# Feed-forward activations turned by 32x32 blocks on VectorE and two DMAs through DRAM instead of on TensorE

## The chip, the cores and the metric

The kernel runs on one core of one Trainium2 chip. The metric is the time of one execution on the device in microseconds (us). A core has TensorE (PE, matrix multiplication, with weight loads listed as PEld), VectorE (DVE), ScalarE (ACT), GpSimd (POOL) and SyncE (SP); each runs its instructions in the order in which the program wrote them, and waits on semaphores where it needs what another engine or a transfer (DMA) delivers. The memories on the core are SBUF (128 partitions) and PSUM (eight banks of 128x512 fp32, into which TensorE writes).

## The reference

Two transformer blocks of width 2048 over 256 tokens, fp32 throughout, within tight tolerances. Attention, a recurrence and the rest of the blocks are cut here; the change touches the two feed-forward parts. Both have 5632 inner features:

```python
# first block
gate, up = jnp.split(h @ w_gate_up[layer], 2, axis=-1)
x = x + rms_norm((jax.nn.silu(gate) * up) @ w_down[layer], g_ffn_post[layer])
...
def conv_ffn(h, w_up, conv_w, conv_b, w_down):     # second block, CONV_WIDTH = 3, L = 256 tokens
    ...
    u = h @ w_up
    up = jnp.pad(u, ((0, 0), (CONV_WIDTH - 1, 0), (0, 0)))
    acc = conv_b
    ...
        acc = acc + conv_w[j] * up[:, j:j + L]
    ...
    return (jax.nn.silu(gate) * val) @ w_down
```

## The kernel before

**Matrix products.** The tokens are two tiles of 128 (t = 0, 1). A product of activations with a weight is cut into chunks of 512 output columns. Its weight comes from DRAM in half-pieces of 512 KB (two blocks of 128 rows by 512 columns), which SP's queue loads into a staging tile `stg`. Fp32 accuracy comes from splitting each operand into a high and a low part: ACT casts the high part of the half-piece into a tile of the `ring` (L278), DVE subtracts it from the staged weight and writes the low part (L285), and PE runs 12 matmuls of 128x512 on it (L331): two blocks, three passes (high by high, high by low, low by high), two token tiles. The activations are stored transposed (features on partitions, tokens along the row), since TensorE contracts over the partitions; the result in PSUM has tokens on the partitions. So between the up product and the down product the activation has to be turned.

**Feed-forward part of the first block.** `ffn` runs gate and up chunks in turn, 11 of each, in six groups: the four chunks of acts 0 and 1, those of acts 2 and 3, then the down product of group 0 (four chunks), then the next group, and so on. `ffn_gate` writes silu of the gate to SBUF; `ffn_up` multiplies the up result with it on DVE (L1017), one 128x512 tile per token tile. Four PE transposes of 128x128 (`transposes`, L346) put the turned tile into a PSUM bank of class `sd`; `evac_split` takes it from there as high part (ACT, L352) and low part (DVE, L353).

**Feed-forward part of the second block.** `ffn2` has the same groups with 22 chunks `conv` (gate and value for each of 11 acts). `two` evacuates both token tiles of a chunk to SBUF on ACT (L1214). Then `conv` fills two `sd` banks with four PE transposes each (L1534), and does the convolution along the row of tokens: ACT writes one tap and the bias (L1541), DVE adds the other two taps (L1542, L1543). Gate chunks end with a Silu on ACT (L1546). Value chunks are multiplied with the gate on Pool (L1560), cast on ACT (L1563), and the low part is subtracted on Pool (L1564).

**What sets the order.** One planner writes the program. It lists all matmul steps with planned times, and before each step it issues the casts of the half-pieces that fall due within 12 us (`AHEAD_HI`), the subtractions within 11 us (`AHEAD_LO`), and the loads that have a staging place. The work between products is written as generators that advance by one `yield` per 1.4 us of planned time (`TICK`); `yield 3` waits for three ticks. So the order on each engine is fixed by planned times, and at run time semaphores alone decide. The down chunk's step waits in the plan until its activation is marked ready. Transfers other than weights go out on Pool's queue (`self.mq`). Small tiles of 128x512 (`s2`) are quarters of pages in SBUF. During act 1's gate chunk of the first feed-forward part a generator `prep_t5` loads two small tables (L483, L484), multiplies them on PE (L486) and spreads the result over 2 MB of DRAM (L490).

Of the kernel before, what the change touches and what calls it, by code (L numbers as in the profile page):

```python
# [8 lines left out]
F32 = mybir.dt.float32  # L9
# [9 lines left out]
P = 128  # L19
# [16 lines left out]
B_LEAD = ((1, 2), (4, 3), (3, 3))  # L36
B_STEP = 2
LO_LAG = 2
NEG = -1.0e30
EPS = 1e-6  # L40

# [38 lines left out]
class Core:  # L80
# [267 lines left out]
    def evac_split(self, bank, hi, lo, scale=None):  # L348

        nc = self.nc  # L350
        if scale is None:
            nc.scalar.copy(hi, bank)  # L352
            nc.vector.tensor_tensor(lo, bank, hi.bitcast(F32), op=ALU.subtract)  # L353
        else:
            nc.scalar.activation(hi, bank, AF.Copy, scale=scale)
            nc.vector.scalar_tensor_tensor(lo, bank, scale, hi.bitcast(F32), op0=ALU.mult, op1=ALU.subtract)

    def x_block(self, src, xt, j, t, goff):

# [16 lines left out]
        def low():  # L376
            yield LO_LAG
            for a in range(4):
                nc.vector.scalar_tensor_tensor(lo[:, a], b3[:, a], g[a], hi[:, a].bitcast(F32), op0=ALU.mult, op1=ALU.subtract)  # L379
            self.put("sd")  # L380
            xt.ready.add((j, t))
# [627 lines left out]
    def ffn_up(self, c, i):  # L1009
        ps = c.ps  # L1010
        nc = self.nc

        def done(t):
            while (i, t) not in self.half:
                yield 1
            g = self.half.pop((i, t))
            nc.vector.scalar_tensor_tensor(g, ps[t], self.rs[t], g, op0=ALU.mult, op1=ALU.mult)  # L1017
            self.put("mm")
            a = self.act[i]
            yield 1  # L1020
            if a.blk[0] is None:
                a.blk[0] = True
                a.blk[0] = yield from self.get("s8", dt=F32R)
            while a.blk[0] is True:
                yield 1
            yield 2
            bank = yield from self.get("sd")
            self.transposes(bank, [g[:, b * P : (b + 1) * P] for b in range(4)])
            self.drop(g)
            s = slice(t * P, (t + 1) * P)  # L1030
            self.evac_split(bank.rearrange("p (k n) -> p k n", k=4), a.hi(0)[:, :, s], a.lo(0)[:, :, s])
            self.put("sd")
            a.ready.add((0, t))
        return done

# [238 lines left out]
    def topk(self):  # L1274
# [11 lines left out]
        for t in range(2):  # L1286
# [3 lines left out]
            for it in range(8):  # L1290
# [3 lines left out]
                if it % 2:  # L1294
                    yield 1
            nc.vector.tensor_scalar(wk, wk, -3.0e38, -NEG, op0=ALU.is_equal, op1=ALU.mult)
            nc.vector.tensor_scalar(wk, wk, NEG, None, op0=ALU.add)
            nc.vector.tensor_tensor(wk[:, n - P : n], wk[:, n - P : n], self.cm[:, P:256], op=ALU.add)
# [225 lines left out]
    def conv(self, c, i, gate):  # L1524
        nc = self.nc
        b0 = 4 * i + (0 if gate else 44)

        def then(got):
            outs = []
            for a in range(2):  # L1530
                bank = yield from self.get("sd")
                for b in range(2):
                    for t in range(2):
                        nc.tensor.transpose(bank[:, (2 * b + t) * P : (2 * b + t + 1) * P],  # L1534
                                            got[t][:, (2 * a + b) * P : (2 * a + b + 1) * P], self.ident)
                o = yield from self.get("s2")
                for b in range(2):
                    k = b0 + 2 * a + b
                    w = [self.cols[:, C_CW + 88 * z + k : C_CW + 88 * z + k + 1] for z in range(3)]
                    u, v = bank[:, 256 * b : 256 * b + 256], o[:, 256 * b : 256 * b + 256]  # L1540
                    nc.scalar.activation(v, u, AF.Identity, scale=w[2], bias=self.cols[:, C_CB + k : C_CB + k + 1])  # L1541
                    nc.vector.scalar_tensor_tensor(v[:, 1:], u[:, 0:255], w[1], v[:, 1:], op0=ALU.mult, op1=ALU.add)  # L1542
                    nc.vector.scalar_tensor_tensor(v[:, 2:], u[:, 0:254], w[0], v[:, 2:], op0=ALU.mult, op1=ALU.add)  # L1543
                self.put("sd")
                if gate:
                    nc.scalar.activation(o, o, AF.Silu)  # L1546
                    self.half[i, a] = o
                outs.append(o)
                yield 1
            self.drop(got[0], got[1])  # L1550
            if gate:
                return
            act = self.act[i]
            act.blk[0] = yield from self.get("s8", dt=F32R)
            for a in range(2):
                while (i, a) not in self.half:
                    yield 1
                g = self.half.pop((i, a))
                o = outs[a]
                nc.gpsimd.tensor_tensor(o, o, g, op=ALU.mult)  # L1560
                o3 = o.rearrange("p (k n) -> p k n", k=2)
                hi, lo = act.hi(0)[:, 2 * a : 2 * a + 2, :], act.lo(0)[:, 2 * a : 2 * a + 2, :]
                nc.scalar.copy(hi, o3)  # L1563
                nc.gpsimd.tensor_tensor(lo, o3, hi.bitcast(F32), op=ALU.subtract)  # L1564
                self.drop(o, g)
                yield 1
            act.ready |= {(0, 0), (0, 1)}
        return self.two(c, then)

    def last_out(self, c, j):  # L1570
# [360 lines left out]
def _pieces(np, w, n=512):  # L1931
    k = w.shape[0]
    return np.ascontiguousarray(w.reshape(k // 256, 2, 128, -1, n).transpose(3, 0, 2, 1, 4))


def _shape_constants(np):
# [12 lines left out]
    c_pick = np.concatenate(picks + [u == pos], axis=1).astype(np.float32)  # L1949
    ninf = np.float32(NEG)  # L1950
    prev = np.where(pos > u, np.float32(0), ninf)
# [15 lines left out]
def _layout(np, a):  # L1967
    heads = [0, 4, 1, 5, 2, 6, 3, 7, 8, 12, 9, 13, 10, 14, 11, 15]
    w_in = a["w_in"][0]
    aq = w_in[:, 0:1024].reshape(2048, 16, 64)[:, heads].reshape(2048, 1024)  # L1970
    w2 = a["w_in_2"][0]

    def cols(v):
        return v.reshape(-1, 128).T

    conv_w = a["conv_w_2"][0]
    vectors = [a["g_mix_pre"][0], a["g_ffn_pre"][0], a["g_ple_pre"][0], a["norm1_g_2"][0], a["norm2_g_2"][0],
               a["kv_norm_g_2"][0], a["hgrn_gnorm"][0], a["conv_b_2"][0], conv_w[0], conv_w[1], conv_w[2]]
    r = {
        "x": a["x"][0], "p": a["p"][0, 0], "pos": np.ascontiguousarray(a["positions"][0].reshape(2, 128).T),  # L1980
        "cols": np.concatenate([cols(v) for v in vectors], axis=1),
        "rv": np.concatenate([a["attn_sinks"][0][heads], a["fgate_b_2"][0]]),
        "lbl": np.ascontiguousarray(a["hgrn_lb_logits"].reshape(2, 8, 128).transpose(2, 0, 1).reshape(128, 16)),
        "w_in": _pieces(np, np.concatenate([aq, w_in[:, 1024:]], axis=1)),
        "w_ab": _pieces(np, a["w_attn_branch"][0].reshape(16, 64, 2048)[heads].reshape(1024, 2048)),
        "w_hb": _pieces(np, a["w_hgrn_branch"][0]),
        "w_out": _pieces(np, a["w_out"][0]),
        "w_gu": _pieces(np, a["w_gate_up"][0]),
        "w_dn": _pieces(np, a["w_down"][0]),
        "w_pg": _pieces(np, a["w_ple_gate"][0]),  # L1990
        "w_pp": _pieces(np, a["w_ple_proj"][0]),
        "w_in2": _pieces(np, np.concatenate([w2[:, 0:1024], w2[:, 1280:2304], w2[:, 2384:5456]], axis=1)),
        "w_sm": _pieces(np, np.concatenate([w2[:, 1024:1280], w2[:, 2304:2384], w2[:, 5456:5464]], axis=1), 344)[0],
        "w_uk": _pieces(np, a["w_uk_2"][0].transpose(2, 0, 1).reshape(256, 1024)),
        "w_uv": _pieces(np, a["w_uv_2"][0].transpose(1, 0, 2).reshape(256, 1024)),
        "w_o": _pieces(np, a["w_o_2"][0]),
        "w_up2": _pieces(np, a["w_up_2"][0]),
        "w_dn2": _pieces(np, a["w_down_2"][0]),
        "g_mix_post": a["g_mix_post"][0], "g_ffn_post": a["g_ffn_post"][0], "g_ple_post": a["g_ple_post"][0],
        "g_fin": a["final_g_2"], "t5": a["t5_table_2"],  # L2000
    }
    r.update(_shape_constants(np))
    return {k: np.ascontiguousarray(v) for k, v in r.items()}
# [16 lines left out]
```

## Time and profile before

| | us |
|---|---|
| three runs | 2701.66, 2703.8, 2704.35 |
| median of the runs | 2703.8 |
| profiled execution, its own time | 2698.83 |
| span of the profiled execution | 2696.8 |

The core's mean granted TensorE clock over the span was 0.997 of full speed. The profile lists each engine's busy time; a group of instructions is one line of the program with one form, and `out<-in` are the program's tiles (`mm` and `sd` are PSUM banks, `s` a tile in SBUF, `ring` the split weights, `stg` the staged ones, names that begin with `d_` are DRAM). The first feed-forward part lies at 707 to 1380 us, the second at 1950 to 2640 us.

### The profile page before, as it was taken

To read this page: it belongs to the slowest core of one execution; us is meant where nothing else is said; L and a number is where in the kernel's file an instruction comes from. 1 tells how busy PE (TensorE), PEld (TensorE's weight loads), DVE (VectorE), ACT (ScalarE), POOL (GpSimd) and SP (SyncE) were. 2 spreads that over 40 slices of the span, in tenths; PEclk is the share of its full clock that TensorE was granted. 3 is DMA by queue.
4 is the path that set the end of the run, shared out by engine and by line. 5 is a ranking of instruction groups with operands and counts; after the bars stand their busy time and mean duration, and the time that the engine had idled before them with its cause. 6 is when DMAs were issued, how large, how long until landed. Compare 5 with 4: busy or idle time off the path is not lost. (4 is left out here: it accounts for less than half of the span.)

```text
span 2696.8 us, 32408 instructions
## 1 busy us (share of the span) xinstructions
PE 2656.7 (99%) x12193; PEld 2194.9 (81%) x12193; DVE 1559.6 (58%) x2063; ACT 1310.5 (49%) x1916; POOL 312.5 (12%) x298
## 2 busy tenths in 40 slices
PE   8999999999999999999999999999999999999998
PEld 7887788888778888888887778788888888888887
DVE  6865675465635445454557564855555646464656
ACT  6545644454525443434345564555455535353634
POOL 1341031021200000000002310100001101020101
PEclk9999999999999999999999999999999999999999
DMA  7445446667576555555557555455555555555553
GB/s 252 164 144 165 152 154 200 218 230 262 197 182 227 191 195 193 193 197 193 192 176 241 206 211 179 146 178 198 187 181 189 185 189 185 190 194 181 195 180 132
DMA packets 144539, 513.97 MB, mean 191 GB/s; under 512 B 17688, under 2 KB 20272, under 8 KB 143360
## 3 DMA queue, kind: packets, MB, share of 16 engines
q1 hardware_dynamic: 133504, 476.83, 51.0%
q0 software_dynamic: 9584, 34.50, 4.2%
q8 instruction: 95, 1.56, 0.2%
q10 hardware_dynamic: 1296, 0.59, 0.1%
q14 instruction: 60, 0.49, 0.1%
HBM read 497.16 MB, written 14.70 MB: 190 GB/s over the span
## 5 line engine op out<-in xcount | busy, mean ns | idle before, releaser
L331 PE MATMUL mm<-ring,s 128*128 128x512 f32 (+1 forms) x10824 | 2526.3, 392 | 4.1 <-ACT s L373 4.1
L331 PEld LDWEIGHTS mm<-ring,s 128*128 128x128 f32 x10824 | 2018.8, 188 | 424.2 <-issue 7.1
L285 DVE TENSOR_TENSOR ring<-stg,ring 128x1024 fp32r<-128x1024 f32 x896 | 1090.7, 1263 | 477.8 <-ACT ring L278 469.4
L278 ACT CAST ring<-stg 128x1024 fp32r<-128x1024 f32 (+1 forms) x904 | 905.1, 1050 | 186.0 <-PE mm L331 68.0
L352 ACT CAST s<-sd 128x512 fp32r<-128x512 f32 (+2 forms) x56 | 28.9, 516 | 225.7 <-PE sd L346 187.9
L1214 ACT ACTIVATE s<-mm,ss 128x512 f32<-128x512 f32 x60 | 41.5, 692 | 198.7 <-PE mm L331 186.0
L1051 DVE TENSOR_TENSOR s<-mm,s 128x512 f32<-128x512 f32 x72 | 48.9, 688 | 107.8 <-PE mm L331 107.8
L1560 POOL TENSOR_TENSOR s<-s,s 128x512 f32<-128x512 f32 x22 | 40.5, 1841 | 583.1 <-DVE s L1543 583.1
L1541 ACT ACTIVATE s<-sd,cols 128x256 f32<-128x256 f32 x88 | 48.6, 563 | 96.0 <-DVE s L1543 61.8
L1542 DVE SCALAR_TENSOR_TENSOR s<-sd,cols,s 128x255 f32<-128x255 f32 x88 | 42.4, 482 | 83.0 <-ACT s L1541 82.4
L1017 DVE SCALAR_TENSOR_TENSOR s<-mm,ss,s 128x512 f32<-128x512 f32 x22 | 16.4, 750 | 110.6 <-PE mm L331 110.6
L1004 ACT ACTIVATE s<-mm,ss 128x512 f32<-128x512 f32 x22 | 15.2, 691 | 132.0 <-PE mm L331 130.8
L346 PE MATMUL sd<-ident,s 128*128 128x128 f32 x340 | 54.6, 284 | 21.3 <-DVE s L975 7.2
L346 PEld LDWEIGHTS sd<-ident,s 128*128 128x128 f32 x340 | 43.2, 146 | 36.1 <-issue 10.2
L353 DVE TENSOR_TENSOR s<-sd,s 128x512 fp32r<-128x512 f32 (+2 forms) x56 | 33.9, 605 | 65.6 <-ACT s L352 65.6
L1064 POOL DMA_DIRECT2D s<-in_p_dram x2 | 1.1, 550 | 603.8 <-PE mm L331 603.8
L799 POOL TENSOR_TENSOR s<-s,s 128x512 f32<-128x512 f32 x32 | 53.1, 1668 | 94.0 <-ACT s L796 89.3
L373 ACT ACTIVATE s<-sd,cols 128x128 fp32r<-128x128 f32 x160 | 45.7, 383 | 30.4 <-PE sd L346 27.5
L341 POOL TENSOR_TENSOR small<-small,mhalf 128x1 f32<-128x1 f32 (+1 forms) x27 | 22.3, 825 | 310.7 <-DVE small L340 278.2
L379 DVE SCALAR_TENSOR_TENSOR s<-sd,cols,s 128x128 fp32r<-128x128 f32 x160 | 44.2, 342 | 10.6 <-ACT s L373 10.6
L1543 DVE SCALAR_TENSOR_TENSOR s<-sd,cols,s 128x254 f32<-128x254 f32 x88 | 42.4, 481 | 3.1
L800 DVE TENSOR_TENSOR s<-s,s 128x512 f32<-128x512 f32 x32 | 32.2, 1027 | 11.5 <-ACT s L796 11.5
(290 smaller groups left out, 1121.6 us busy)
## 6 DMA issues: line engine op xcount, KB each, us to landing
stg<-in_w_in_dram SPq DMA_DIRECT2D x232, 512.0 KB, 4.4
stg<-in_w_gu_dram SPq DMA_DIRECT2D x176, 512.0 KB, 5.3
stg<-in_w_dn_dram SPq DMA_DIRECT2D x176, 512.0 KB, 5.2
stg<-in_w_up_dram SPq DMA_DIRECT2D x176, 512.0 KB, 5.0
stg<-in_w_out_dram SPq DMA_DIRECT2D x32, 512.0 KB, 5.4
stg<-in_w_pg_dram SPq DMA_DIRECT2D x32, 512.0 KB, 5.6
stg<-in_w_o_dram SPq DMA_DIRECT2D x32, 512.0 KB, 4.7
stg<-in_w_hb_dram SPq DMA_DIRECT2D x16, 512.0 KB, 4.9
```

Of the source, the lines that this page charges most:

```text
L278: nc.scalar.copy(w[:, 0, :, 0 : cc.n], stg[n_hi][0][:, :, 0 : cc.n])
L285: eng.tensor_tensor(wl[:, :, 0 : cc.n], unstage(n_lo)[:, :, 0 : cc.n], wh[:, :, 0 : cc.n].bitcast(F32), op=ALU.subtract)
L331: nc.tensor.matmul(c.ps[t][:, 0 : c.n], xl if p == "C" else xh, wl if p == "B" else wh, start=n == 0, stop=n == 6 * c.nhp - 1)
L346: self.nc.tensor.transpose(bank[:, a * P : (a + 1) * P], s, self.ident)
L373: nc.scalar.activation(hi[:, a], b3[:, a], AF.Copy, scale=g[a])
L379: nc.vector.scalar_tensor_tensor(lo[:, a], b3[:, a], g[a], hi[:, a].bitcast(F32), op0=ALU.mult, op1=ALU.subtract)
L799: nc.gpsimd.tensor_tensor(k3, d3, kt[:, None, :].to_broadcast([P, 4, P]), op=ALU.mult)
L1051: nc.vector.tensor_tensor(y, ps[t], y, op=ALU.add)
L1214: nc.scalar.activation(r, ps[t], AF.Copy, scale=self.rs[t])
L1541: nc.scalar.activation(v, u, AF.Identity, scale=w[2], bias=self.cols[:, C_CB + k : C_CB + k + 1])
L1542: nc.vector.scalar_tensor_tensor(v[:, 1:], u[:, 0:255], w[1], v[:, 1:], op0=ALU.mult, op1=ALU.add)
L1543: nc.vector.scalar_tensor_tensor(v[:, 2:], u[:, 0:254], w[0], v[:, 2:], op0=ALU.mult, op1=ALU.add)
```

## The change

Between the product and the split, the tile no longer goes through TensorE. `flip_out` lets DVE transpose each 32x32 block of the 128x512 tile in place of its own block and writes the tile to DRAM (256 KB, Pool's queue). Three ticks later `flip_in` reads it back so that partition 4r+j holds, for each of the four 32-row stripes, the 128 columns of quarter j (four pieces of 512 bytes per partition). Five ticks after that the tile is used. In this layout the features of a block of 512 lie on the partitions in another order, and the tokens in runs of 32; the views in `ffn_up` and `conv` put the tokens in order, and the host lays out the down weights' rows, the convolution's taps and its bias in the features' new order. `ffn_up` splits straight from SBUF. `conv` first copies the two token tiles on ACT into one tile `bank` in SBUF (L1562 of the kernel after), and convolves from there. In the kernel after the lines are numbered 3 to 26 higher: casts L281, subtractions L288, matmuls L334, block transposes L365, DMAs out L369 and in L375, the evacuation of `two` L1235, Identity L1567, taps L1568 and L1569, Silu L1572, product L1586, casts L1589, low parts L1590.

```diff
--- before.py
+++ after.py
@@ -36,6 +36,9 @@
 B_LEAD = ((1, 2), (4, 3), (3, 3))
 B_STEP = 2
 LO_LAG = 2
+FLIPS = 8
+FLIP_OUT = 3
+FLIP_IN = 5
 NEG = -1.0e30
 EPS = 1e-6
 
@@ -354,6 +357,23 @@
         else:
             nc.scalar.activation(hi, bank, AF.Copy, scale=scale)
             nc.vector.scalar_tensor_tensor(lo, bank, scale, hi.bitcast(F32), op0=ALU.mult, op1=ALU.subtract)
+
+    def flip_out(self, src):
+
+        nc = self.nc
+        ts = yield from self.get("s2")
+        nc.vector.transpose(ts, src)
+        self.drop(src)
+        self.serial += 1
+        d = self.dram.tile([P, 512], F32, tag="flip", bufs=FLIPS, name=f"flip_{self.serial}")
+        self.mq.dma_start(d, ts)
+        return ts, d
+
+    def flip_in(self, d):
+
+        tr = yield from self.get("s2")
+        self.mq.dma_start(tr.rearrange("p (i x) -> p i x", i=4), d.rearrange("(i r) (j x) -> (r j) i x", i=4, j=4))
+        return tr
 
     def x_block(self, src, xt, j, t, goff):
 
@@ -1017,19 +1037,20 @@
             nc.vector.scalar_tensor_tensor(g, ps[t], self.rs[t], g, op0=ALU.mult, op1=ALU.mult)
             self.put("mm")
             a = self.act[i]
-            yield 1
+            ts, d = yield from self.flip_out(g)
+            yield FLIP_OUT
+            tr = yield from self.flip_in(d)
+            self.drop(ts)
             if a.blk[0] is None:
                 a.blk[0] = True
                 a.blk[0] = yield from self.get("s8", dt=F32R)
             while a.blk[0] is True:
                 yield 1
-            yield 2
-            bank = yield from self.get("sd")
-            self.transposes(bank, [g[:, b * P : (b + 1) * P] for b in range(4)])
-            self.drop(g)
+            yield FLIP_IN
             s = slice(t * P, (t + 1) * P)
-            self.evac_split(bank.rearrange("p (k n) -> p k n", k=4), a.hi(0)[:, :, s], a.lo(0)[:, :, s])
-            self.put("sd")
+            hi, lo = (z[:, :, s].rearrange("p a (i q) -> p a i q", q=32) for z in (a.hi(0), a.lo(0)))
+            self.evac_split(tr.rearrange("p (i a q) -> p a i q", i=4, a=4), hi, lo)
+            self.drop(tr)
             a.ready.add((0, t))
         return done
 
@@ -1526,14 +1547,19 @@
         b0 = 4 * i + (0 if gate else 44)
 
         def then(got):
-            outs = []
+            outs, ds, trs = [], [], []
+            for t in range(2):
+                ds.append((yield from self.flip_out(got[t])))
+            yield FLIP_OUT
+            for ts, d in ds:
+                trs.append((yield from self.flip_in(d)))
+                self.drop(ts)
+            yield FLIP_IN
             for a in range(2):
-                bank = yield from self.get("sd")
-                for b in range(2):
-                    for t in range(2):
-                        nc.tensor.transpose(bank[:, (2 * b + t) * P : (2 * b + t + 1) * P],
-                                            got[t][:, (2 * a + b) * P : (2 * a + b + 1) * P], self.ident)
-                o = yield from self.get("s2")
+                bank, o = yield from self.get("s2", 2)
+                b4 = bank.rearrange("p (b t i q) -> p b t i q", b=2, t=2, i=4)
+                for t in range(2):
+                    nc.scalar.copy(b4[:, :, t], trs[t].rearrange("p (i a q) -> p a i q", i=4, a=4)[:, 2 * a : 2 * a + 2])
                 for b in range(2):
                     k = b0 + 2 * a + b
                     w = [self.cols[:, C_CW + 88 * z + k : C_CW + 88 * z + k + 1] for z in range(3)]
@@ -1541,13 +1567,13 @@
                     nc.scalar.activation(v, u, AF.Identity, scale=w[2], bias=self.cols[:, C_CB + k : C_CB + k + 1])
                     nc.vector.scalar_tensor_tensor(v[:, 1:], u[:, 0:255], w[1], v[:, 1:], op0=ALU.mult, op1=ALU.add)
                     nc.vector.scalar_tensor_tensor(v[:, 2:], u[:, 0:254], w[0], v[:, 2:], op0=ALU.mult, op1=ALU.add)
-                self.put("sd")
+                self.drop(bank)
                 if gate:
                     nc.scalar.activation(o, o, AF.Silu)
                     self.half[i, a] = o
                 outs.append(o)
                 yield 1
-            self.drop(got[0], got[1])
+            self.drop(*trs)
             if gate:
                 return
             act = self.act[i]
@@ -1973,9 +1999,12 @@
     def cols(v):
         return v.reshape(-1, 128).T
 
-    conv_w = a["conv_w_2"][0]
+    def flip(w):
+        return np.ascontiguousarray(w.reshape(-1, 4, 4, 32, *w.shape[1:]).swapaxes(1, 2).swapaxes(2, 3)).reshape(w.shape)
+
+    conv_w = flip(a["conv_w_2"][0].T).T
     vectors = [a["g_mix_pre"][0], a["g_ffn_pre"][0], a["g_ple_pre"][0], a["norm1_g_2"][0], a["norm2_g_2"][0],
-               a["kv_norm_g_2"][0], a["hgrn_gnorm"][0], a["conv_b_2"][0], conv_w[0], conv_w[1], conv_w[2]]
+               a["kv_norm_g_2"][0], a["hgrn_gnorm"][0], flip(a["conv_b_2"][0]), conv_w[0], conv_w[1], conv_w[2]]
     r = {
         "x": a["x"][0], "p": a["p"][0, 0], "pos": np.ascontiguousarray(a["positions"][0].reshape(2, 128).T),
         "cols": np.concatenate([cols(v) for v in vectors], axis=1),
...
-        "w_dn": _pieces(np, a["w_down"][0]),
+        "w_dn": _pieces(np, flip(a["w_down"][0])),
...
-        "w_dn2": _pieces(np, a["w_down_2"][0]),
+        "w_dn2": _pieces(np, flip(a["w_down_2"][0])),
```

The instructions move as follows. On PE, at a gate chunk of the second feed-forward part (`mm` the chunk's two PSUM banks, `ring` its half-pieces, `s` the activations or, with `ident`, the evacuated tile), before:

```order
L331 MATMUL mm_14499<-ring_14422,s_1267_13211 128x512 x6
L331 MATMUL mm_14508<-ring_14422,s_1267_13211 128x512 x6
L331 MATMUL mm_14499<-ring_14438,s_1267_13211 128x512 x6
L1534 MATMUL sd_14523<-ident,s_1377_14486 128x128 x4
L331 MATMUL mm_14508<-ring_14438,s_1267_13211 128x512 x6
L1534 MATMUL sd_14543<-ident,s_1377_14486 128x128 x4
L331 MATMUL mm_14499<-ring_14454,s_1282_13374 128x512 x6
L331 MATMUL mm_14508<-ring_14454,s_1282_13374 128x512 x6
```

and in the kernel after:

```order
L334 MATMUL mm_14485<-ring_14385,s_1267_13189 128x512 x6
L334 MATMUL mm_14494<-ring_14385,s_1267_13189 128x512 x6
L334 MATMUL mm_14485<-ring_14401,s_1267_13189 128x512 x6
L334 MATMUL mm_14494<-ring_14401,s_1267_13189 128x512 x6
L334 MATMUL mm_14485<-ring_14425,s_1282_13352 128x512 x6
L334 MATMUL mm_14494<-ring_14425,s_1282_13352 128x512 x6
```

The eight transposes that stood among the first matmuls of the following chunk are gone, and the matmuls stand in the same order.

On DVE at the same chunk (subtractions of weights, then the taps of the convolution), before:

```order
L285 TENSOR_TENSOR ring_14488<-stg_4614,ring_14488 128x1024
L285 TENSOR_TENSOR ring_14506<-stg_121,ring_14506 128x1024
L1542 SCALAR_TENSOR_TENSOR s_1377_14486<-sd_14523,cols,s_1377_14486 128x255
L1543 SCALAR_TENSOR_TENSOR s_1377_14486<-sd_14523,cols,s_1377_14486 128x254
L1542 SCALAR_TENSOR_TENSOR s_1377_14486<-sd_14523,cols,s_1377_14486 128x255
L1543 SCALAR_TENSOR_TENSOR s_1377_14486<-sd_14523,cols,s_1377_14486 128x254
L1542 SCALAR_TENSOR_TENSOR s_1377_14486<-sd_14543,cols,s_1377_14486 128x255
L1543 SCALAR_TENSOR_TENSOR s_1377_14486<-sd_14543,cols,s_1377_14486 128x254
L1542 SCALAR_TENSOR_TENSOR s_1377_14486<-sd_14543,cols,s_1377_14486 128x255
L1543 SCALAR_TENSOR_TENSOR s_1377_14486<-sd_14543,cols,s_1377_14486 128x254
```

and in the kernel after, from the two block transposes to the first taps:

```order
L365 STREAM_TRANSPOSE s_1377_14472<-s_1377_14472 128x512 x2
L288 TENSOR_TENSOR ring_14515<-stg_121,ring_14515 128x1024
L288 TENSOR_TENSOR ring_14531<-stg_126,ring_14531 128x1024
L288 TENSOR_TENSOR ring_14549<-stg_126,ring_14549 128x1024
L288 TENSOR_TENSOR ring_14565<-stg_4611,ring_14565 128x1024
L1568 SCALAR_TENSOR_TENSOR s_1377_14472<-s_1377_14472,cols 128x255
L1569 SCALAR_TENSOR_TENSOR s_1377_14472<-s_1377_14472,cols 128x254
L1568 SCALAR_TENSOR_TENSOR s_1377_14472<-s_1377_14472,cols 128x255
L1569 SCALAR_TENSOR_TENSOR s_1377_14472<-s_1377_14472,cols 128x254
```

The taps now stand four subtractions behind the block transposes and read SBUF instead of `sd`.

On Pool's queue at acts 0 and 1 of the first feed-forward part (`c_hot` and `t` are the small tables of `prep_t5`, `d_t` the 2 MB), before:

```order
L994 DMA d_x<-s_475_4618 128x2048
L483 DMA s_516_5058<-in_c_hot_dram 32x512
L484 DMA s_516_5058<-in_t_dram 32x8
L490 DMA d_t_88<-s_516_5058 1024x1x512
L1064 DMA s_883_9342<-in_p_dram 128x256
```

and in the kernel after:

```order
L1014 DMA d_x<-s_475_4618 128x2048
L369 DMA flip_5583<-s_516_5058 128x512
L369 DMA flip_5595<-s_516_5058 128x512
L503 DMA s_516_5058<-in_c_hot_dram 32x512
L504 DMA s_516_5058<-in_t_dram 32x8
L375 DMA s_562_5609<-flip_5583 128x4x128
L375 DMA s_516_5058<-flip_5595 128x4x128
L510 DMA d_t_88<-s_516_5058 1024x1x512
L369 DMA flip_5868<-s_572_5733 128x512
L369 DMA flip_5880<-s_572_5733 128x512
```

The two writes of act 0's tiles now stand ahead of the tables' loads, and their two reads ahead of the 2 MB write; act 1's two writes stand behind it.

## Rows read from the trace of the kernel before

**Rows 1.** Page, busy time by engine: us, share of the span, instructions.
```profile
PE 2656.7 (99%) x12193; PEld 2194.9 (81%) x12193; DVE 1559.6 (58%) x2063; ACT 1310.5 (49%) x1916; POOL 312.5 (12%) x298
```

**Rows 2.** Stretches: us, busy PE, PEld, DVE, ACT, POOL; granted clock, DMA share, GB/s.
```profile
707.00:1380.00 673.00, 670.01 (x2996) 553.36 (x2997) 331.67 (x342) 274.17 (x328) 9.32 (x14) 1.00 0.57 195
1950.00:2640.00 690.00, 690.00 (x3134) 571.57 (x3133) 398.14 (x467) 343.02 (x432) 76.16 (x48) 1.00 0.54 186
...
801.50:804.90 3.40, 3.36 (x12) 2.69 (x13) 0.64 (x1) 0.19 (x1) 0.00 (x0) 0.57 0.77 173
```

**Rows 3.** Timeline of PE in the second feed-forward part: start, duration, count.
```profile
2072.81 15.58 PE L331 MATMUL mm<-ring,s 128*128 128x512 f32 x68
2088.23 0.60 PE L1534 MATMUL sd<-ident,s 128*128 128x128 f32 x4
2088.58 1.64 PE L331 MATMUL mm<-ring,s 128*128 128x512 f32 x6
2090.06 0.60 PE L1534 MATMUL sd<-ident,s 128*128 128x128 f32 x4
...
```

**Rows 4.** Groups by line and form, PE: busy us, mean ns | idle before.
```profile
L346 PE MATMUL sd<-ident,s 128*128 128x128 f32 x340 | 54.6, 284 | 21.3 <-DVE s L975 7.2 <-DMA ident<-in_c_ident_dram 4.1 <-DMA s<-in_x_dram 3.4
...
L1534 PE MATMUL sd<-ident,s 128*128 128x128 f32 x176 | 26.3, 272 | 0.0
```

**Rows 5.** Timeline, first feed-forward part, act 1: in brackets wait and releaser.
```profile
798.52 1.05 ACT L278 CAST ring<-stg 128x1024 fp32r<-128x1024 f32 x1 [5.18 <-DMA stg<-in_w_gu_dram]
...
800.74 1.40 DVE L1017 SCALAR_TENSOR_TENSOR s<-mm,ss,s 128x512 f32<-128x512 f32 x2
...
801.54 0.76 PE L346 MATMUL sd<-ident,s 128*128 128x128 f32 x4 [2.54 <-DVE s L1017]
...
801.95 2.91 PE L331 MATMUL mm<-ring,s 128*128 128x512 f32 x6
```

**Rows 6.** DMA transfers: queue, count, KB each, median us from issue to landing.
```profile
d_gate<-s POOLq DMA_DIRECT2D x16, 256.0 KB, 2.6
...
s<-d_gate POOLq DMA_DIRECT2D x16, 256.0 KB, 5.7
...
s<-d_t POOLq DMA_DIRECT2D x1, 512.0 KB, 5.5
...
d_t<-s POOLq DMA_DIRECT2D x1, 2048.0 KB, 46.1
```

**Rows 7.** Landings of the sixteen 256 KB reads of L885, read with Rows 6.
```profile
DMA to landing us min/median/max: 3.6/5.7/8.4
```

**Rows 8.** Groups by line and form, DVE, ACT and Pool: columns as in Rows 4.
```profile
L285 DVE TENSOR_TENSOR ring<-stg,ring 128x1024 fp32r<-128x1024 f32 x888 | 1084.2, 1267 | 475.5 <-ACT ring L278 467.1 <-issue 7.8
L278 ACT CAST ring<-stg 128x1024 fp32r<-128x1024 f32 x896 | 899.6, 1052 | 186.0 <-PE mm L331 68.0 <-DMA stg<-in_w_gu_dram 34.8 <-DMA stg<-in_w_in_dram 21.5
...
L1051 DVE TENSOR_TENSOR s<-mm,s 128x512 f32<-128x512 f32 x72 | 48.9, 688 | 107.8 <-PE mm L331 107.8
L1543 DVE SCALAR_TENSOR_TENSOR s<-sd,cols,s 128x254 f32<-128x254 f32 x88 | 42.4, 481 | 3.1
L1214 ACT ACTIVATE s<-mm,ss 128x512 f32<-128x512 f32 x60 | 41.5, 692 | 198.7 <-PE mm L331 186.0 <-issue 12.7
L1560 POOL TENSOR_TENSOR s<-s,s 128x512 f32<-128x512 f32 x22 | 40.5, 1841 | 583.1 <-DVE s L1543 583.1
...
L1546 ACT ACTIVATE s<-s 128x512 f32<-128x512 f32 x22 | 13.9, 633 | 23.7 <-DVE s L1543 23.7
...
L1339 ACT ACTIVATE s<-s,small 128x256 f32<-128x256 f32 x16 | 8.0, 502 | 3.6 <-DVE small L1334 3.6
```

**Rows 9.** Landing of the transfer of `c_hot` (L483), issued at 731.3 us.
```profile
L483 POOL DMA_DIRECT2D s<-in_c_hot_dram x1: 525/525/525, 731.3 to 731.3; - x1
...
DMA to landing us min/median/max: 9.8/9.8/9.8
```

**Rows 10.** Timeline at the small tables: act 0's product and the table's matmul.
```profile
752.12 0.75 DVE L1017 SCALAR_TENSOR_TENSOR s<-mm,ss,s 128x512 f32<-128x512 f32 x1 [0.61 <-PE mm L331]
...
761.04 1.02 PE L486 MATMUL sd<-s 32*8 32x512 f32 x2
```

## The prediction

> **What bounds the kernel now.** I read the page's busy times first: PE is busy for 99% of the span, DVE 58%, ACT 49% [rows 1]. An average over stages does not say where the change works, so I took the two feed-forward stretches: PE is busy 670.01 of 673.00 us in the first and 690.00 of 690.00 in the second, at a granted clock of 1.00 (2.4 GHz), with the transfers at 0.57 and 0.54 [rows 2]. The reader is to see that PE never waits there, with one exception below. So what leaves PE's queue shortens the span, and what is added to DVE, ACT and Pool is free as long as it does not make PE wait.
>
> **Removed: the PE transposes.** Twenty-two tiles in the first part (11 acts, two token tiles) and 44 banks in the second (22 chunks, two each) make 66 groups of four. A transpose is listed with 272 to 284 ns [rows 4], but they overlap with their neighbours. In the timeline 68 matmuls take 2088.23 - 2072.81 = 15.42 us, 0.2268 each, and from one group of transposes to the next, with six matmuls between, pass 2090.06 - 2088.23 = 1.83 us [rows 3]. 1.83 - 6 x 0.2268 = 0.47 us per group: 66 x 0.47 = 31.0 us on the path.
>
> The Trainium skill ("TensorE: Matmul & The Clock Gate", Part 4: PE-mode transpose) gives a transpose of 128x128 about 275 ns within a kernel. The listed duration agrees with that figure; the distance of the group's neighbours, 0.47 us for four, does not, and the path goes by the distance.
>
> **Added: the chain of a conv chunk.** Call T the end of a chunk's matmuls and count from there. The evacuation of the second tile takes 0.69 [rows 8], say 0.8 until the block transposes start. No DVE block transpose is in the trace. Nearest rows: one PSUM operand of 128x512 in 0.69 (L1051), and twice that size in 1.27 (L285) [rows 8]; I take 0.69, 1.27 is the dear end. Two of them 1.4; the write of 256 KB lands 2.6 after its issue, a read of 256 KB after 5.7, a read in pieces of 512 bytes after 5.5 for twice the size [rows 6]. The second read is issued behind the first write's landing and one more issue, at 4.1, so the flip lasts 9.8 us; with the fastest read of L885, 3.6, it lasts 7.7, with the slowest, 8.4, it lasts 12.5 [rows 7].
>
> From the landing X on, the work is in order on ACT and DVE. In a gate chunk ACT does two copies and two Identities of 128x256 at 0.50 each (the nearest row is L1339), waits some 1.4 for the last taps (0.48 each, L1543), does Silu 0.63 and a cast 1.05, then copies, Identities and taps again: 2.0 + 1.4 + 0.63 + 1.05 + 2.0 + 1.4 = 8.5. Then DVE subtracts the weight that stood behind the taps (1.27): done at X + 9.8. ACT goes on with Silu, cast, evacuation, cast, evacuation, cast (0.63 + 3 x 1.05 + 2 x 0.69 = 5.2, to 13.7), and behind the last cast comes DVE's subtraction, then the next chunk's block transposes: at X + 14.9 [rows 8]. A value chunk has no Silu ahead of the taps (8.5 - 2.0 = 6.5 and 7.7 for its first subtraction), and comes to X + 13.1 with the casts behind Pool's product of 1.84 [rows 8].
>
> So gate plus value take 9.8 + 14.9 + 9.8 + 13.1 = 47.6 us in this loop, and PE needs 2 x 96 x 0.2268 = 43.5 us for the two chunks. The loop is slower, by 2.9 in a gate chunk and 1.1 in a value chunk. What hides that is the weights' lead: the first subtraction behind the taps belongs to the half-piece that PE reaches ten half-pieces after T, 10 x 12 x 0.2268 = 27.2. The start of the block transposes after T goes 0.8, 3.7, 4.8, 7.7 over four chunks; the fourth is done at 7.7 + 9.8 + 7.7 = 25.2, still ahead of 27.2. Down chunks then give 16 half-pieces (43.5 us) in which the loop rests. But ahead of the first down chunks stand eight conv chunks. In chunks 5 to 8 the subtraction is late by 1.3, 0.7, 3.3 and 0.7: +6.0 us. With a flip of 7.7 this is 0; with 11.3 every group of four stalls, about 28 us in all; with 12.5 about 50.
>
> A stall also costs clock: behind the wait of 2.54 us at 801.5 the granted clock was 0.57 for 3.4 us, and six matmuls took 2.91 in place of 1.36 [rows 2, 5]. One of the four stalls is as long: +1.5.
>
> **The first feed-forward part.** There the plan leaves 8 ticks of 1.4, 11.2 us, between the up product and the split, against a flip of 9.8 from its first transpose, and the down product that needs the result begins at least one chunk of 21.8 us later. I cost it at nothing, except at two places. At 801.5 PE waits 2.54 us in transposes for the up product on DVE, since DVE stood behind a cast that waited 5.18 for weights [rows 5], while the 2 MB write (46.1 to land) took the transfers [rows 6]. This cost 2.54 + 1.55 + 0.16 (the transposes took 0.76, elsewhere 0.60 [rows 3]) = 4.3. The wait goes with the transposes, but the weights are as late as before, and PE meets them in the ring. Bounds 0 to 10; I take 6.0, a little above what it cost: +1.7.
>
> The other place is the small table: its load moves behind act 0's two writes on Pool's queue. The writes follow the up product, 752.12 + 0.75 [rows 10], with two block transposes: issued by 754.5, landed 9.8 later as before [rows 9] at 764.3, while PE wants it at 760.1: at 761.04 [rows 10] less act 0's two groups of transposes, 2 x 0.47, which no longer stand ahead. Bounds 0 (landed in 5.7, as the reads of rows 6) to 4.5; taken +1.0.
>
> **The transfers.** 132 more of 256 KB are 34.6 MB, spread over both parts, where the share was 0.57 and 0.54 [rows 2]; I cost them at nothing beyond the flip's own length. If they slow the weights, it shows as casts that wait for `stg`.
>
> **The sum.** 2698.8 - 31.0 + 6.0 + 1.5 + 1.7 + 1.0 = 2678.0 for the profiled execution. The median of the runs, 2703.8, stands 5.0 above the profiled 2698.8: 2683.
>
> **Rivals.**
> A, the forecast: PE keeps the bound, 2683; its own range goes from 2668.5 (no stall in the loop, none at 801, none at the table: 2698.8 - 31.0 - 4.3 + 5.0) to 2692 (flip 10.5).
> B, the loop gives back half: flip between 10.5 and 11.3, 2690 to 2703. For it: a chunk's two writes and two reads go out together, while the median was taken over single pairs.
> C, the other side: the reads' landing decides. From a flip of 11.3 on, the conv loop costs more than the transposes saved; at 12.5 it is 2683 - 7.5 + 50 = 2725. For it: the slowest of sixteen like reads took 8.4 [rows 7], and ACT and DVE stand still for weights while they wait. Against it: the median was 5.7 with the weights streaming as they do here.
> D, each transpose saves its listed time: 264 x 0.272 = 71.8 [rows 4], 2683 - 71.8 + 31.0 = 2642. The distances in [rows 3] deny it. This is what the figure of the Trainium skill's Part 4 above would make of it.
> E, the read is slow of itself because of its pieces: if it lands as late as the 2 MB write, 46.1 [rows 6], each of 22 conv chunks loses 46.1 - 5.7 = 40.4, 2683 + 889 = 3572. The 512 KB in pieces of 512 bytes that landed in 5.5 [rows 6] speak against it. The Trainium skill ("VectorE: DVE Perf Modes", The three transpose paths) warns that a plain DMA that transposes by strides is 19 times slower than the DMA's own transpose where the innermost destination stride is large; 19 x 5.7 = 108 us per read would give above 4000, an estimate from that page. Here the innermost 512 bytes lie together on both sides.
> F, the change does not do what it says to the bound: PE takes the freed time as waits for weights, about 2703.
>
> **Chances.** A 0.60, B 0.15, C 0.17, D 0.02, E 0.02, F 0.04. The likeliest is A: 2683. The range 2667 to 2706 takes in A, B, F and the near edge of C, about 0.78. What a measurement of this kernel can tell from no change is 0.2%, 5.4 us, so between 2698.4 and 2709.2. Faster: A, D and most of B, 0.75; same: the rest of B, F and an edge of C, 0.07; slower: 0.18.
>
> **What would show it.** PE has 264 transposes fewer (12193 to 11929 instructions), and between conv chunks its matmuls follow at 0.2268 without the 0.47. L365 lasts about 0.69; the flip's write lands in about 2.6, its read in 5.7; ACT's copies L1562 wait for it. PE's few waits lie in front of L334 in the second to fourth act of the second part (some 6 us), with the ring's subtraction as releaser, and none later. The step that would be wrong first is the flip's length: above 11.3 the copies' waits push the casts, and PE waits in every group of four. The second is the duration of L365, the third the loss of clock behind each wait, if there are many.

## The result and the profile after

The changed kernel takes 2763.61 us (median of 4 runs, 2761.55 to 2765.79) against 2704.07 before: 1.0218 times the time, 95% interval 1.0200 to 1.0236. It is slower by 59.5 us, where 2683 was forecast. Its profiled execution has a span of 2759.8.

The page of the kernel after, busy time by engine, and the chain of work that ended last by engine, as in [rows 1]:

```profile
PE 2661.1 (96%) x11929; PEld 2187.3 (79%) x11929; DVE 1609.4 (58%) x2129; ACT 1341.6 (49%) x2004; POOL 399.1 (14%) x430
...
PE 23%; DMA 8%; DVE 6%; issue 5%; ACT 4%; POOL 1%; ACTq 0%; POOLq 0%; DVEq 0%
```

The second of these lines on the page of the kernel before:

```profile
PE 44%; DVE 1%; issue 1%; ACT 0%; ACTq 0%; POOLq 0%; POOL 0%; DVEq 0%
```

The 264 transposes are gone (12193 to 11929), and yet PE is busy for 4 us longer. The page follows the chain back over some 47% of the span in both kernels. Nearly all of that was PE's; now half of it runs through transfers, DVE and ACT, so PE alone no longer sets the time. The groups by line and form of the kernel after (busy us, mean ns | idle before, who ended it) say where:

```profile
L334 PE MATMUL mm<-ring,s 128*128 128x512 f32 x10728 | 2528.6, 396 | 65.2 <-DVE ring L288 51.9 <-ACT ring L281 9.0 <-ACT s L393 4.1
...
L365 DVE STREAM_TRANSPOSE s<-s 128x512 f32<-128x512 f32 x66 | 45.5, 703 | 1.9
...
L1562 ACT COPY s<-s 128x256 f32<-128x256 f32 x88 | 33.5, 404 | 226.3 <-DMA s<-flip 219.4 <-DVE s L1569 6.9
```

The line of before that answers to the first:

```profile
L331 PE MATMUL mm<-ring,s 128*128 128x512 f32 x10728 | 2511.0, 393 | 4.1 <-ACT s L373 4.1
```

The matmuls of `mm` waited for 4.1 us in all; now they wait for 65.2, mostly for the weights' low parts. They also run longer, 17.6 us over all 10,728 (2528.6 - 2511.0), at a lower granted clock (below). In the kernel after ACT waits 219 us in front of its copies for the tiles that come back.

The stretch of the second feed-forward part in the kernel after (columns as in [rows 2]) shows both: PE is idle for 54 of 780 us, and the clock is 0.96 where it was 1.00.

```profile
1940.00:2720.00 780.00, 725.62 (x3085) 591.73 (x3084) 447.02 (x523) 381.13 (x531) 135.53 (x140) 0.96 0.58 200
```

Counting off matmuls places the loss. I set the start of every 96th matmul of the two traces side by side, counting all 10,824 matmuls into `mm`. Up to matmul 2640 the two differ by 0.7 to 2.3 us, as executions of one kernel do. In the first part, matmuls 2736 to 3264 (which hold the transposes of acts 0 to 2) lose 6.8, and the 2,304 behind them gain 7.6, by 0.94 at each pair of transposed groups. In the second part matmul 7680 starts at 1954.3 and 1956.0, and matmul 10752, shortly before the end of its last down chunk, at 2671.3 and 2734.4: 61.4 us lost, although its 22 chunks save 22 x 0.94 = 20.7. So its stalls are worth 82 us: the 54 in which PE stands idle, and some 28 by which its matmuls run longer at the lower clock.

One value chunk of the kernel after, timeline with the wait and its releaser in brackets:

```profile
2164.53 1.52 DVE L365 STREAM_TRANSPOSE s<-s 128x512 f32<-128x512 f32 x2
2164.64 5.14 SPq L257 DMA_DIRECT2D stg<-in_w_dn_dram  x4
2165.53 0.56 POOL L369 DMA_DIRECT2D flip<-s  x1 [17.91 <-DVE s L365]
...
2166.35 0.56 POOL L369 DMA_DIRECT2D flip<-s  x1 [0.26 <-DVE s L365]
...
2171.19 0.76 POOL L375 DMA_DIRECT2D s<-flip  x1 [4.29 <-issue]
...
2172.60 0.76 POOL L375 DMA_DIRECT2D s<-flip  x1 [0.65 <-DMA flip<-s]
2177.52 0.41 ACT L1562 COPY s<-s 128x256 f32<-128x256 f32 x1 [8.84 <-DMA s<-flip]
2180.23 0.41 ACT L1562 COPY s<-s 128x256 f32<-128x256 f32 x1 [2.30 <-DMA s<-flip]
...
2181.30 0.48 DVE L1568 SCALAR_TENSOR_TENSOR s<-s,cols,s 128x255 f32<-128x255 f32 x1 [8.41 <-ACT s L1567]
```

From the first block transpose to the last landing pass 15.7 us (2164.5 to 2180.2), and for 11 of them ACT stands in front of the copies, with every later cast behind it. The four weight loads that begin at 2164.64 go out together with the two writes.

How long the transfers took to land, in the second part (first two lines writes, then reads) and, last two lines, the writes in the first part:

```profile
L369 POOL DMA_DIRECT2D flip<-s x44: 557/562/602, 1975.0 to 2691.2; - x44
DMA to landing us min/median/max: 3.6/5.1/6.3
...
L375 POOL DMA_DIRECT2D s<-flip x44: 759/759/787, 1980.4 to 2697.1; - x44
DMA to landing us min/median/max: 4.7/6.6/7.6
...
L369 POOL DMA_DIRECT2D flip<-s x22: 544/557/581, 754.9 to 1380.6; - x22
DMA to landing us min/median/max: 2.3/2.3/11.2
```

The same write of 256 KB lands in 2.3 us in the first part and in 5.1 in the second. Over the 22 chunks of the second part the flip took 14.3 us at the median (12.9 to 15.7), where the forecast had 9.8.

### The profile page after: what moved, and what is told of

It reads as the page before. It is cut to its first block, busy times and chain, and to the rows that moved or that the text cites. A ratio compares the mean times of both kernels' runs of the same rounds, so it can differ in the third digit from the quotient of the medians.

```text
span 2759.8 us, 32445 instructions
## 1 busy us (share of the span) xinstructions
PE 2661.1 (96%) x11929; PEld 2187.3 (79%) x11929; DVE 1609.4 (58%) x2129; ACT 1341.6 (49%) x2004; POOL 399.1 (14%) x430
## 5 line engine op out<-in xcount | busy, mean ns | idle before, releaser
L334 PE MATMUL mm<-ring,s 128*128 128x512 f32 (+1 forms) x10824 | 2544.0, 395 | 65.2 <-DVE ring L288 51.9
L334 PEld LDWEIGHTS mm<-ring,s 128*128 128x128 f32 x10824 | 2042.1, 190 | 506.3 <-DVE ring L288 61.4
L288 DVE TENSOR_TENSOR ring<-stg,ring 128x1024 fp32r<-128x1024 f32 x896 | 1094.2, 1267 | 361.7 <-ACT ring L281 360.8
L281 ACT CAST ring<-stg 128x1024 fp32r<-128x1024 f32 (+1 forms) x904 | 904.3, 1049 | 159.2 <-DMA stg<-in_w_gu_dram 48.4
L369 POOL DMA_DIRECT2D flip<-s x66 | 37.2, 564 | 987.4 <-DVE s L365 987.1
L1562 ACT COPY s<-s 128x256 f32<-128x256 f32 x88 | 33.5, 404 | 226.3 <-DMA s<-flip 219.4
L1568 DVE SCALAR_TENSOR_TENSOR s<-s,cols,s 128x255 f32<-128x255 f32 x66 | 33.5, 507 | 133.9 <-ACT s L1567 133.9
L1235 ACT ACTIVATE s<-mm,ss 128x512 f32<-128x512 f32 x60 | 41.2, 686 | 128.2 <-PE mm L334 115.5
L355 ACT CAST s<-s 128x512 fp32r<-128x512 f32 x22 | 13.7, 621 | 161.4 <-DMA s<-flip 125.7
L375 POOL DMA_DIRECT2D s<-flip x66 | 50.2, 762 | 124.9 <-DMA flip<-s 70.3
L819 POOL TENSOR_TENSOR s<-s,s 128x512 f32<-128x512 f32 x32 | 53.3, 1672 | 94.5 <-ACT s L816 89.7
L1568 DVE SCALAR_TENSOR_TENSOR s<-s,cols 128x255 f32<-128x255 f32 x22 | 10.6, 481 | 94.8 <-ACT s L1567 94.8
L355 ACT CAST s<-sd 64x256 fp32r<-64x256 f32 (+2 forms) x34 | 16.0, 470 | 86.2 <-PE sd L349 48.2
L1567 ACT ACTIVATE s<-s,cols 128x256 f32<-128x256 f32 x88 | 48.1, 594 | 1.5
```

The costliest lines, as they stand in the source:

```text
L281: nc.scalar.copy(w[:, 0, :, 0 : cc.n], stg[n_hi][0][:, :, 0 : cc.n])
L288: eng.tensor_tensor(wl[:, :, 0 : cc.n], unstage(n_lo)[:, :, 0 : cc.n], wh[:, :, 0 : cc.n].bitcast(F32), op=ALU.subtract)
L334: nc.tensor.matmul(c.ps[t][:, 0 : c.n], xl if p == "C" else xh, wl if p == "B" else wh, start=n == 0, stop=n == 6 * c.nhp - 1)
L375: self.mq.dma_start(tr.rearrange("p (i x) -> p i x", i=4), d.rearrange("(i r) (j x) -> (r j) i x", i=4, j=4))
L819: nc.gpsimd.tensor_tensor(k3, d3, kt[:, None, :].to_broadcast([P, 4, P]), op=ALU.mult)
L1562: nc.scalar.copy(b4[:, :, t], trs[t].rearrange("p (i a q) -> p a i q", i=4, a=4)[:, 2 * a : 2 * a + 2])
```

## The experiments

The theory: the flip stops ACT, which works in order, and DVE behind it; the weights' casts and subtractions that stand behind come late, and PE waits. Rival 1: the added traffic slows the weights. Rival 2: the added work of ACT and DVE is what makes the loop long.

**One part at a time.** In the first kernel `ffn_up` and the rows of `w_dn` are those of before, in the second `conv`, its taps, bias and `w_dn2` (shown as edits of the kernel after, one line of each):

```diff
-        "w_dn": _pieces(np, flip(a["w_down"][0])),        # e1: and ffn_up of before
+        "w_dn": _pieces(np, a["w_down"][0]),
...
-        "w_dn2": _pieces(np, flip(a["w_down_2"][0])),     # e2: and conv, conv_w, conv_b of before
+        "w_dn2": _pieces(np, a["w_down_2"][0]),
```

> Only the second feed-forward part takes the new way; the first turns its tiles on PE as before. Theory (the flip, 14.3 us at the median there in place of 9.8, stops ACT and DVE in order, and the weights' casts behind them come late): 20.7 us of transposes saved and some 82 us of stalls, before + 61 = 2765. Rival 1 (the 34.6 MB of transfers slow the weights wherever they run): two thirds of 60, before + 40 = 2744. Rival 2 (ACT's and DVE's added work in the convolution makes the loop long): 2765 as well.

> Only the first feed-forward part takes the new way. Theory: 10.3 us of transposes saved, against 8.7 + 2.5 lost at acts 0 and 1 (weights behind the 2 MB write; the small table behind the flips): before + 1, 2705 within 3. Rival 1 (transfers slow the weights): a third of 60, 2724. Rival 2: 2694, since that loop isn't in it.

The second part alone: 2776.29 (one execution) against 2704.22; between matmuls 7680 and 10752 it loses 65.5; in the profiled execution 12 more lie at places that this kernel shares with before (6.1 ahead of matmul 2640, 1.7 at acts 0 to 2, 4.3 between the parts). The first part alone: 2699.7 (10 executions), ratio 0.9984, interval 0.9974 to 0.9993: 4.5 faster where I expected 1 slower. The stretch of acts 0 to 2 loses 3.3 there and not 6.8; this place varies. So but for that stretch the loss lies in the second part, and rival 1, which wanted 20 us in the first, falls. Rival 2 expected 2765 and 2694 here and is not ruled out yet.

**The wait taken away, with and without the traffic.** What follows reads the tile that DVE transposed; in the second kernel the transfers are left out too. The edit in `conv` (in `ffn_up` it is the same):

```diff
-                trs.append((yield from self.flip_in(d)))
-                self.drop(ts)
+                waste.append((yield from self.flip_in(d)))      # e3; left out in e4
+                trs.append(ts)
```

> Both parts flip and all 132 transfers are made, but what follows reads the tile that DVE transposed and not the one that came back (the features' exchange between stripes is left out of the result). Theory: no wait for the flip is left, the traffic and the added work stay: 2704 - 31 + up to 8 (weights and small table at acts 0 and 1) = 2673 to 2682. Rival 1 (traffic): 2764. Rival 2 (added work): 2764.

> As the run without the wait, and the 132 transfers are left out too. Theory: 2673 to 2680, within 5 of the run with the transfers. Rival 1 (traffic): 2675, but then the run with the transfers is far slower. Rival 2 (added work): 2764.

2668.49 with the traffic, below the window that I had given, and 2676.02 without (one execution each). The groups of the kernel without the wait, PE and ACT:

```profile
L334 PE MATMUL mm<-ring,s 128*128 128x512 f32 x10728 | 2493.4, 392 | 6.0 <-ACT s L393 4.1 <-DVE ring L288 1.9
...
L1562 ACT COPY s<-s 128x256 f32<-128x256 f32 x88 | 31.3, 404 | 50.3 <-DVE s L1569 50.3
```

PE waits no longer, with all 132 transfers and all of ACT's and DVE's added work in place: both rivals are refuted, and the whole saving is there. Against this kernel PE waits 59 us longer in front of these matmuls in the kernel after (65.2 and 6.0), and they run 35 us longer (2528.6 and 2493.4); together that is about the 93 between the two spans (2759.8 and 2666.7). In the second part both kernels gain the 20.7 to a tenth of a microsecond. Nearly all of the 7.5 between them lie outside the feed-forward parts (4.4 ahead of matmul 2640, 3.0 between the parts), where the two kernels do the same.

**More time between write, read and use.**

```diff
-FLIP_OUT = 3
-FLIP_IN = 5
+FLIP_OUT = 5        # e6: 6
+FLIP_IN = 8         # e6: 12
```

> The reads are issued five ticks after the writes and used eight ticks after that (3 and 5 before), so that 6 to 7 casts stand between the block transposes and the copies, and not 4. Theory (ACT stops in order for a flip that is longer than what stands between): the stop is mostly gone, 14.3 + 9.6 against a chunk of 21.8 leaves some lateness; 2672 to 2700. Rival (the flip's loop from product to product is too long whatever stands in it): 2764.

> Six and twelve ticks: the copies of a chunk now stand behind the evacuations of the next chunk, so two flips are under way at once. Theory: no stop is left, also at act 1 of the first part, whose flip took 20.4; 2704 - 31 - 4 = 2669, 2664 to 2676. Rival (the loop is too long): 2764. Rival (traffic): excluded by the run without the wait, would be 2764.

2671.53 (one execution, just below the window) and 2671.0 (4 executions, 2670.35 to 2674.58, against 2702.79; ratio 0.9883, interval 0.9866 to 0.9899). So the change does pay, by 1.2%, once little or nothing stands still for the flip. With 5 and 8 ticks ACT's copies still wait 22.9 us for transfers, and the second part gains 16.5 of its 20.7. With 6 and 12 ticks the groups of PE and ACT read:

```profile
L334 PE MATMUL mm<-ring,s 128*128 128x512 f32 x10728 | 2497.3, 392 | 6.8 <-ACT s L393 4.7 <-DVE ring L288 2.1
...
L1562 ACT COPY s<-s 128x256 f32<-128x256 f32 x88 | 31.3, 405 | 11.7 <-DVE s L1569 9.2 <-DVE s L365 1.6 <-ACT ring L281 0.8
```

The copies never wait for a transfer, though a flip there lasts up to 22 us. The stretch of acts 0 to 2 gains 7.0 instead of losing 6.8, the second part gains its 20.7.

**A flip of the assumed length.** The reads of the second part fetch the tiles of the chunk before:

```diff
-            for ts, d in ds:
+            old = getattr(self, "old", None) or ds
+            self.old = ds
+            for (ts, _), (_, d) in zip(ds, old):
```

> The kernel after, but in the second feed-forward part the reads fetch the tiles that the chunk before wrote, so that they need not wait for this chunk's writes (wrong tiles are convolved). The flip is then some 9.5 to 10 us, about the length that the prediction assumed, at the same order and the same traffic. Theory: the prediction's recurrence was right and only the flip's length wrong, so the second part costs 7.5 of stalls against 20.7 saved; with the first part as after, 2692, between 2684 and 2700. Rival (the work in the loop was underestimated too): above 2715.

2714.05, above the window and just under the rival's. But the flip did not become 9.5 to 10 throughout: the second read of a value chunk still went out 6 to 8 us after the block transposes, and the flips took 12.5 at the median (10.0 to 14.2). The second part lost 12.1, that is 33 of stalls. The prediction's recurrence, fed with the 22 flips as measured, gives 45 here, and 92 for the kernel after, where 82 were measured. So it runs 10 to 12 us too high in both, and the work in the loop was not underestimated. The recurrence has no term for the clock; it can be held only against the sum of waiting and slower matmuls.

**Earlier block transposes.** To see why the writes take 5 us in the second part:

```diff
-    def two(self, c, then):
+    def two(self, c, then, lag=3):
...
-                yield 3
+                if lag:
+                    yield lag
...
-        return self.two(c, then)          # at the end of conv
+        return self.two(c, then, 0)
```

> The kernel after, but in the second feed-forward part the block transposes follow the evacuation at once and not three ticks later, so that one or two of the weights' subtractions that free staging places stand behind them and not ahead. Theory on the write (it lands in 4.8 and not in 2.3 because a burst of weight loads, released by those subtractions, shares the transfer engines with it): the writes land in under 3.5 at the median, the flip is 12 to 13, and the time is 2700 to 2745. Rival (two writes within 0.6 us hinder each other, or the second part's tiles land late anyhow): the writes still take 4.8, the flip 14, the time 2755 or more.

2774.78 (one execution), and the writes still landed in 5.2 at the median. That is what the rival had said; but the edit did not do what I meant, so it does not decide between the two. At the first chunk of all and at those behind down chunks, where the loop is not late, the write landed in 2.3; at the others the burst had moved along, as this timeline of the run shows:

```profile
2112.39 8.55 SPq L257 DMA_DIRECT2D stg<-in_w_up_dram  x7
...
2114.55 1.52 DVE L365 STREAM_TRANSPOSE s<-s 128x512 f32<-128x512 f32 x2
...
2115.55 0.56 POOL L369 DMA_DIRECT2D flip<-s  x1 [18.63 <-DVE s L365]
```

Seven loads of 512 KB go out from 3 us ahead of the write to 5 us behind it, as ACT and DVE catch up after a stop and free the staging places one after the other. Across the runs the landing goes with the weight loads on the transfer engines. Stretches behind a write in the kernel after, in the second part and in the first (DMA share is the last column but one):

```profile
2165.50:2170.50 5.00, 5.00 (x24) 4.14 (x23) 5.00 (x6) 3.17 (x4) 1.11 (x2) 1.00 0.90 305
857.00:859.50 2.50, 2.50 (x12) 2.06 (x11) 2.46 (x4) 0.00 (x0) 1.09 (x2) 1.00 0.29 113
```

and in the run with 5 and 8 ticks, in the second part:

```profile
2013.90:2016.40 2.50, 2.50 (x13) 2.07 (x12) 1.39 (x2) 0.00 (x0) 2.48 (x3) 1.00 0.50 179
```

These three writes landed in 5.1, 2.3 and 2.36 us. In the last stretch no weight load moved; its share is that of the two writes. I took the first write of each pair in six traces (the kernel after, the two with one part alone, 5 and 8 ticks, 6 and 12 ticks, the older tile), 165 in all, and the share of the transfer engines' time that weight loads had in the two microseconds behind its issue: below a tenth, all 64 landed in 2.29 to 2.71; above a half, 94 landed in 3.3 to 9.4, with 4.2 to 5.7 for the busiest eight; the seven between took 2.9 to 11.2, four of them behind the 2 MB write. Rival, that two writes 0.6 to 0.8 us apart hinder each other: with 5 and 8 ticks such a pair landed in 2.36 and 2.94, and in the run with the early block transposes five pairs landed in 2.31 to 2.36 each, so no. The link to the loads is a correlation; I made no run that holds the loads back and leaves the rest. The stop is not needed for it: without the wait, and with 6 and 12 ticks, where no copy waits for a transfer, the weight loads also had more than half of that time behind 21 of the 22 first writes of the second part. These writes landed in 3.6 and 4.2 at the median (4.8 in the kernel after), and the flips took 13.7 and 13.8.

## Why the prediction was wrong

**The step that failed** is "the flip lasts 9.8 us". Its terms against the measured ones: two block transposes 1.4, measured 1.3 to 1.5 (0.703 each); the write 2.6, measured 5.1; the read 5.7, measured 6.6. With the second issue behind the first it comes to 14.3. The 2.6 was the median of the writes of `d_gate`, most of which had few weight loads behind them; in the second part the loads go out together with the writes, with a stop or without one. They are the likely cause, from the correlation above; no run shows it by itself. Of the 83.5 by which the profiled execution (2761.55) stands above the forecast 2678.0, this term makes 82 - 7.5 = 75.

**The mechanism was named, and given 0.17.** Rival C said that from 11.3 us on the loop costs more than the transposes save, which is what happened. With 14.3 the recurrence gives 93 of stalls and 2683 - 7.5 + 93 = 2769; measured 2763.6. The bound of 12.5 was too low: it stretched the read and left the write at its median. Worked again, the recurrence gives 30 and 54 at a flip of 11.3 and 12.5, where the prediction has 28 and 50; and the chances of A, B and F alone add up to 0.79, not 0.78. Neither slip changes the outcome.

**The saving** was right: 0.47 us per group of four, 0.94 per chunk wherever PE doesn't wait, 31.0 in all. By the 275 ns of the Trainium skill ("TensorE: Matmul & The Clock Gate", Part 4: PE-mode transpose) it would have been some 73, an estimate worked out from that page. The run without the wait does not bear that out: it was 35.7 faster than before, which is about the 31.0 and the 4.3 at act 1.

**Small terms.** The table cost nothing instead of 1.0: its matmul stands at number 2820, and from matmul 2784 to 2880 the kernel after gains 0.94, all that its two groups of transposes save. A copy takes 0.404 where 0.50 was assumed, an Identity 0.594 against 0.50; taps that read SBUF 0.48 to 0.61 against 0.48.

**Acts 0 and 1.** Matmuls 2736 to 3264 lost 6.8 although six groups of transposes were saved there: the stalls grew by 6.8 + 6 x 0.47 = 9.6, in place of the +1.7 taken. The reason was wrong too. I left the weights' lateness as the cost. But without the flip's wait the place gains 6.8, which is about the 4.3 that it cost before and the transposes (2.8): the weights alone cost nothing there. What cost is again the wait for the flip, now for a write behind the 2 MB (11.2 to land, flip 20.4). The timeline of the kernel after shows ACT's stop and the two waits of PE behind it, 2.9 of the 6.7 us that PE waits there:

```profile
828.02 0.62 ACT L355 CAST s<-s 128x512 fp32r<-128x512 f32 x1 [5.84 <-DMA s<-flip]
...
829.63 0.49 PE L334 MATMUL mm<-ring,s 128*128 128x512 f32 x1 [0.96 <-ACT ring L281]
...
832.04 14.26 PE L334 MATMUL mm<-ring,s 128*128 128x512 f32 x50 [1.91 <-DVE ring L288]
```

The other 3.8 lie ahead of this stop, at 808.4 to 814.8, behind casts that waited for weights. They too are gone in the run without the wait; how the flip came to delay those weights stays open.

**What I should have read.** The forecast took "in order" into account for the length of the loop, and treated the flip as a term in it. The two numbers that set the order (3 and 5 ticks, 11.2 us of planned time) stood in the diff, and the planned time was only 1.4 longer than the flip that I hoped for. That alone would have widened the upper end. The trace of before also had the slow writes: the sixteen of `d_gate` (L871) landed in 2.3 to 4.8, and the four with weight loads in more than half of the two microseconds behind them took 3.6 to 4.8. I looked at the spread of the reads [rows 7], not at that of the writes.

## What to carry to other kernels

A transfer's latency is free only if the engine that uses the result has other work queued ahead of the use for the whole of that latency; on an engine that works in order, everything behind the wait stands still too. Whether the bound pays for that depends on the slack behind it: in the first part ACT's casts waited 125.7 us for flips, and PE waited for weights only at act 1; in the second, where every chunk flips, PE paid 82 us. So place the use by the slowest landing and not by the median. When a change moves work off the bound and the time rises, first take away the wait and keep the work: here one such run showed that the saving was whole and only the place of the use was wrong.

## What the runs showed of the hardware

A write of 256 KB from SBUF to DRAM landed in 2.3 to 2.7 us when the weight loads left the transfer engines nearly alone (below a tenth of their time), and in 4.8 at the median (3.3 to 9.4) when they held more than half of it; behind the 2 MB write it took 11.2. A DVE transpose of 128x512 by blocks of 32x32 takes 0.703 us, about what another pass of two operands of the same size takes (0.688, L1051 of before [rows 8]). The 34.6 MB of additional traffic did not slow PE at all where nothing waited for it: with 6 and 12 ticks the DMA share of the second part rose from 0.54 to 0.66, and PE was busy throughout:

```profile
1950.00:2640.00 690.00, 690.00 (x3046) 571.32 (x3045) 443.23 (x519) 378.67 (x527) 132.01 (x137) 1.00 0.66 226
```
